# Device layouts, DRAM hops and pooling on VectorE in a hybrid decoder step on eight cores

## The chip, the cores and the metric

The kernel runs on all 8 cores of one Trainium2 chip, two dies of four cores each (cores 0 to 3 and 4 to 7). Every core does the same program on its own share of the batch: one prompt of 2048 tokens and 16 sample sequences of 4 tokens, together 2112 columns. The cores do not talk to each other. The metric is the device time in microseconds of the slowest core.

Executions come in two states. In the fast state all cores have nearly the same granted TensorE clock (0.95 to 0.99 of full speed here). In the slow state one die, or both, is granted less (down to 0.80) and the run takes 1 to 17% longer, whatever the kernel. A ratio is the mean time of one kernel's fast runs over that of the other's fast runs of the same rounds, so it is not quite the ratio of the medians that are quoted beside it.

## The reference, cut to what matters

Four layers. In each, one input projection feeds three branches. Branch A pools over trailing windows of 2, 4, 8 and 16 tokens. Branch B is a spatial gate, u * (W v + b), in chunks of 128 tokens. Branch C is a gated depthwise convolution of width 31 with a LayerNorm. The three are concatenated, go through one output projection, and a gated feed-forward network (FFN) with a depthwise convolution of width 3 follows.

```python
def pool_mix(xa, prev, pos0, w_pool, scale):
    xp = jnp.concatenate([prev, xa], axis=1).astype(jnp.float32)
    cs = jnp.concatenate([zeros, jnp.cumsum(xp, axis=1)], axis=1)
    for g, w in enumerate((2, 4, 8, 16)):                  # 64 channels each
        s = cs[:, P+1:P+1+T, sl] - cs[:, P+1-w:P+1-w+T, sl]
        outs.append(s / jnp.minimum(pos + 1, w))
    pooled = jnp.concatenate(outs, -1) - xp[:, P:]
    out = einsum('btgc,gcd->btgd', pooled, w_pool) * scale
    return out, xp[:, -P:]                                 # the new state: the last 15 rows, an output
# per layer (cut):
    c_in = zc[..., :D_C] * sigmoid(zc[..., D_C:])
    c_conv, cst = causal_dwconv(c_in, conv_prev[l], conv_w[l], conv_b[l])
    c_out = silu(layernorm(c_conv, ...))
    x = x + concat([a_out, b_out, c_out], -1) @ w_out[l]
    x = x + (silu(dwconv3(h2 @ w_gate)) * (h2 @ w_val)) @ w_down[l]
```

The states that a next step needs are outputs too: of pooling (15 rows), of the convolution (30 rows) and of the FFN convolution (2 rows), and the rows of v.

## The kernel before

Everything on the chip has channels on the 128 partitions and tokens in the free dimension. The convolution uses another layout (12 groups, 4 phases of 32 channels), so its input has to hop into that layout and its output back. A helper records every operation with what it reads and writes and places the waits; memory is handed out from one arena in which buffers overlay each other, so an operation can wait for a transfer that still reads the memory that it will overwrite. The parts that the argument touches:

```python
# conv input: 16 transfers from SBUF to SBUF for each third j of the channels
for q in range(4):
    for f in range(4):
        S.dma("sp", Q[32*f:32*f+32, 4*j+q, 8:8+MT], cin[32*q:32*q+32, j, f, :], DQ[j], reads=[Rcin[j]], writes=[Rq[j]])
# ... the last 94 tokens once more, with channels in the free dimension, for the state outputs (TensorE)
for k in range(KC):
    S.op("pe", lambda e: e.matmul(pt[0:94, 0:256], H[:, k, NT-94:NT], wv[:, k, 0:256], ...))        # L561
# ... 12 conv groups, sums for the LayerNorm (L601), LayerNorm on VectorE, with V matmuls (L633) between
# conv output: again 16 small transfers per third, then a GpSimd copy into token order (L671)
for f in range(4):
    S.dma("sp", cop[32*q:32*q+32, j, f, :], coq[32*f:32*f+32, :], DCO[j], reads=[Rys[g]], writes=[Rcp[j]])
# ... pooling: projection A (L718), then the window sum as matmuls of shifted operands (L744), with weights
# that GpSimd scales by the coefficient of each shift (L706): 4 shifts for one half, 16 for the other
for i in range(WMAX[j]):
    S.op("pe", lambda e: e.matmul(pb[:, 0:n], wpb[:, j, i, :], zab[:, j, 15+c0-i:15+c0-i+n], start=(i == 0), ...))
# ... 22 transposes of the FFN state (L782), then the spatial gate and U (L798, L812), then output projection (L838)
# ... FFN: per block of 128 channels, after the two groups of 8 matmuls per token tile (L893, L897), a small one
for k in range(KC):
    S.op("pe", lambda e: e.matmul(pt[0:66, 0:128], H[:, k, NT-66:NT], wv[:, k, 0:128], ...))        # L926
```

Inputs come in the reference's layouts, so x, the vectors and the states are transposed on TensorE at the start and y at the end; the spatial weights are masked and transposed at each layer boundary.

## Time and profile before

The median is 3372.56 us of 3 runs. I cut the slowest core's execution into stages by the start of the first matmul of each kind in the TensorE timeline:

| stage (us) | layer 1 | 2 | 3 | 4 |
|---|---|---|---|---|
| start to first projection | 85.7 | | | |
| conv input projection | 48.0 | 51.1 | 54.0 | 54.0 |
| conv | 48.1 | 48.3 | 47.9 | 48.3 |
| conv end to output projection | 114.4 | 114.0 | 114.2 | 113.9 |
| output projection | 83.1 | 83.1 | 83.1 | 83.1 |
| FFN up to the last down projection | 445.2 | 445.1 | 446.3 | 442.4 |
| last down projection to the next layer, or to the end | 67.4 | 66.5 | 66.7 | 116.6 |

The first lines are from the page of the kernel before: busy microseconds of TensorE with their share of the span, and the share of each engine in the chain of work that ended last.

```profile
PE 3099.0 (92%) x17856; PEld 1516.0 (45%) x17856; DVE 1706.6 (51%) x3064; ACT 1463.8 (43%) x2876; POOL 363.1 (11%) x460
...
PE 81%; DVE 5%; SPq 4%; issue 3%; ACT 2%; DMA 2%; POOL 1%; DVEq 0%; ACTq 0%; POOLq 0%
```

TensorE (PE) is the bound, so time goes only where its instructions or its gaps go. The next lines are the TensorE timeline of the kernel before around the start of the third layer's conv. The columns are start, duration, engine, line, operation, output and inputs, count, and in brackets how long the engine had stood before and what released it.

```profile
1756.38 2.10 PE L608 MATMUL ps<-arena 128*128 128x512 bf16 x9
...
1770.44 1.05 PE L601 MATMUL ps<-arena,oneb 128*128 128x512 bf16 x4 [11.74 <-DVE arena L620]
1771.34 4.00 PE L608 MATMUL ps<-arena 128*128 128x512 bf16 x9
```

TensorE stands 11.74 us, and the next nine matmuls take 4.00 us instead of 2.10: the restart is slow. The release names VectorE, but VectorE only passed on a wait. This is the ScalarE timeline of the same moment, and below it the queue of SyncE, which issues transfers.

```profile
1769.06 0.70 ACT L618 ACTIVATE arena<-ps,cvq_s 128x528 f32<-128x528 f32 x1 [14.30 <-DMA o_conv_s<-arena]
```

```profile
1739.85 25.16 SPq L134 DMA_DIRECT2D arena<-arena  x31
...
1765.68 1.96 SPq L134 DMA_DIRECT2D o_conv_s<-arena  x4
```

ScalarE had to wait for an output transfer that reads memory which it overwrites, and that transfer stood in the queue behind 31 hop transfers of 0.8 us of issue each. Now the stretch between conv and output projection of the third layer, again TensorE:

```profile
1824.32 12.49 PE L718 MATMUL ps<-H,wsall 128*128 128x512 bf16 x64
1844.35 3.94 PE L718 MATMUL ps<-H,wsall 128*128 128x512 bf16 x16 [7.54 <-ACT arena L721]
...
1858.02 16.15 PE L744 MATMUL ps<-arena 128*128 128x512 bf16 x80 [4.47 <-POOL arena L706]
1874.01 0.17 PE L767 MATMUL ps<-arena,pw 128*128 128x16 bf16 x1
...
1875.02 4.64 PE L782 MATMUL ps<-cstt,arena 32*128 32x32 f32 x22
```

The pooling matmuls (L744) and the state transposes (L782) are work that the change takes away, and 12 us are gaps. One more reading: a GpSimd copy and a VectorE operation that ran beside it, from the two engines' timelines.

```profile
1822.79 4.05 POOL L671 COPY arena<-arena 128x2048 bf16<-128x2048 bf16 x1 [32.42 <-DMA arena<-arena]
```

```profile
1823.23 4.18 DVE L657 TENSOR_TENSOR arena<-arena 128x528 f32<-128x528 f32 x1
```

The operation of L657 takes 0.70 us beside no copy. The Trainium skill, page "SBUF — State Buffer", section "Who interferes with whom", says that a VectorE instruction with two inputs in SBUF contends with a GpSimd instruction that reads SBUF; the 4.18 us agree.

### The profile page before, as it was taken

How to read it: one execution, taken by the hardware profiler on the slowest of the kernel's cores; microseconds unless marked ns; L12 is line 12 of the kernel's file. 1: busy time of each engine (PE TensorE's matmuls, PEld its weight loads, DVE VectorE, ACT ScalarE, POOL GpSimd, SP SyncE). 2: the span in 40 equal slices, each digit the busy share in tenths (PEclk: the TensorE clock that was granted, in tenths of full speed). 3: DMA queues.
4: the chain of work that ended last, by engine and by line, in shares of the span. 5: the costliest groups of instructions: out<-in, count | busy, mean ns of one | idle time of the engine just before them, and what ended most of it. 6: DMA issues, size and time to landing. Idle time of an engine off the chain costs nothing.

```text
span 3370.9 us, 53934 instructions; the slowest of 8 cores (3356.4 to 3370.9 us)
## 1 busy us (share of the span) xinstructions
PE 3099.0 (92%) x17856; PEld 1516.0 (45%) x17856; DVE 1706.6 (51%) x3064; ACT 1463.8 (43%) x2876; POOL 363.1 (11%) x460
## 2 busy tenths in 40 slices
PE   4889999999888999999878999999988899999995
PEld 3445444444344444444434544444434454444443
DVE  4234664645532475555543366464652347556455
ACT  4240662725342273545425147272732407536353
POOL 0120001000002010101012101010101200010100
PEclk8899999999998999999989999999998999999998
DMA  5522233333332233333152223333315213333312
GB/s 134 95 44 32 26 40 38 34 39 48 48 65 41 28 33 39 39 39 35 33 85 52 32 26 34 38 40 39 43 25 94 44 22 31 37 35 40 39 27 103
DMA packets 326036, 152.94 MB, mean 45 GB/s; under 512 B 229171, under 2 KB 312071, under 8 KB 325511
## 3 DMA queue, kind: packets, MB, share of 16 engines
q0 software_dynamic: 287232, 108.03, 28.2%
q1 hardware_dynamic: 38535, 41.48, 4.2%
q8 instruction: 151, 2.47, 0.3%
q14 instruction: 118, 0.97, 0.1%
HBM read 232.98 MB, written 14.75 MB: 73 GB/s over the span
## 4 chain that ended last, share of the span: by engine, by line
PE 81%; DVE 5%; SPq 4%; issue 3%; ACT 2%; DMA 2%; POOL 1%; DVEq 0%; ACTq 0%; POOLq 0%
PE ps L893 19%; PE ps L897 18%; PE ps L948 14%; PE ps L838 7%; PE ps L983 5%; SPq L134 4%; PE ps L812 4%; PE ps L608 3%; PE ps L542 2%; DVE H L379 2%; PE ps L546 2%; PE ps L744 2%; PE ps L367 1%; PE ps L926 1%; ACT arena L365 1%
## 5 line engine op out<-in xcount | busy, mean ns | idle before, releaser
L893 PE MATMUL ps<-H,wsall 128*128 128x512 bf16 (+1 forms) x3520 | 703.1, 343 | 0.0
L897 PE MATMUL ps<-H,wsall 128*128 128x512 bf16 (+1 forms) x3520 | 700.2, 342 | 0.0
L910 DVE SCALAR_TENSOR_TENSOR arena<-arena,vt 128x512 f32<-128x512 f32 (+1 forms) x440 | 288.9, 657 | 432.3 <-ACT arena L909 431.9
L905 ACT COPY arena<-ps 128x512 f32<-128x512 f32 (+1 forms) x440 | 224.4, 510 | 650.0 <-PE ps L893 643.6
L948 PE MATMUL ps<-arena,wsall 128*128 128x512 bf16 (+1 forms) x2560 | 458.3, 342 | 0.0
L893 PEld LDWEIGHTS ps<-H,wsall 128*128 128x128 bf16 x3520 | 305.1, 98 | 335.4 <-issue 3.9
L897 PEld LDWEIGHTS ps<-H,wsall 128*128 128x128 bf16 x3520 | 302.1, 98 | 332.3
L365 ACT ACTIVATE arena<-X 128x512 bf16<-128x512 f32 (+1 forms) x360 | 171.7, 543 | 527.8 <-PE ps L367 270.9
L909 ACT ACTIVATE arena<-ps,vt 128x512 f32<-128x512 f32 (+1 forms) x440 | 309.2, 703 | 65.4 <-DVE arena L912 0.9
L948 PEld LDWEIGHTS ps<-arena,wsall 128*128 128x128 bf16 x2560 | 216.1, 98 | 241.6
L951 DVE TENSOR_TENSOR X<-ps,X 128x512 f32<-128x512 f32 (+1 forms) x320 | 185.3, 596 | 257.2 <-PE ps L948 257.2
L912 DVE SCALAR_TENSOR_TENSOR arena<-arena,vt 128x512 f32<-128x512 f32 (+1 forms) x440 | 289.4, 658 | 46.9 <-DVE arena L910 1.4
L134 POOL DMA_DIRECT2D wsall<-w_up x176 | 154.0, 879 | 1231.1 <-PE ps L926 716.5
L919 DVE TENSOR_TENSOR arena<-arena 128x512 bf16<-128x512 bf16 (+1 forms) x440 | 258.9, 591 | 3.0 <-ACT arena L918 2.6
L838 PE MATMUL ps<-arena,wsall 128*128 128x512 bf16 (+3 forms) x1440 | 260.3, 341 | 0.0
L379 DVE SCALAR_TENSOR_TENSOR H<-X,vt,arena 128x512 bf16<-128x512 f32 (+1 forms) x320 | 209.4, 657 | 93.2 <-ACT arena L376 63.6
L915 ACT CAST arena<-ps 128x512 bf16<-128x512 f32 (+1 forms) x440 | 223.9, 509 | 72.1 <-PE ps L897 71.9
L918 ACT ACTIVATE arena<-arena 128x512 f32<-128x512 f32 (+1 forms) x440 | 246.1, 559 | 3.3 <-DVE arena L912 3.1
L983 PE MATMUL ps<-arena,wsall 128*128 128x512 bf16 (+1 forms) x960 | 184.7, 358 | 12.3 <-DVE X L986 9.3
L838 PEld LDWEIGHTS ps<-arena,wsall 128*128 128x128 bf16 (+1 forms) x1440 | 120.0, 97 | 134.1 <-issue 0.2
L367 PE MATMUL ps<-arena,ones 128*128 128x512 bf16 (+1 forms) x360 | 120.7, 375 | 58.7 <-ACT arena L365 39.5
L840 DVE TENSOR_TENSOR X<-ps,X 128x512 f32<-128x512 f32 (+1 forms) x160 | 91.5, 594 | 135.3 <-PE ps L838 130.3
(123 smaller groups left out, 2550.4 us busy)
## 6 DMA issues: line engine op xcount, KB each, us to landing
wsall<-w_up POOLq DMA_DIRECT2D x176, 256.0 KB, 5.0
wsall<-w_down POOLq DMA_DIRECT2D x32, 512.0 KB, 5.6
arena<-cwd POOLq DMA_DIRECT2D x48, 288.0 KB, 6.7
arena<-arena SPq DMA_DIRECT2D x384, 33.0 KB, 1.9
arena<-xp SPq DMA_DIRECT2D x4, 2048.0 KB, 15.1
y_p<-arena SPq DMA_DIRECT2D x16, 512.0 KB, 2.7
wsall<-w_in POOLq DMA_DIRECT2D x24, 256.0 KB, 6.5
wsall<-w_in POOLq DMA_DIRECT2D x8, 768.0 KB, 9.9
```

The costliest lines, as they stand in the source:

```text
L134: ins = st["eng"].dma_start(out=out, in_=in_, **kw)
L379: S.op("dve", lambda e: e.scalar_tensor_tensor(H[:, kc, c0:c0 + n], X[:, kc, c0:c0 + n], VT[:, gcol + kc:gcol + kc + 1], ri, ALU.mult, ALU ...
L838: S.op("pe", lambda e: e.matmul(pb[:, 0:n], lh, rh, start=(q == 0), stop=(q == 8)), reads=[RWS[sl], rr], writes=[Rpb], inc=(q == 8))
L893: S.op("pe", lambda e: e.matmul(pg[:, 0:n], wv[:, k, 0:128], H[:, k, c0:c0 + n], start=(k == 0), stop=(k == 7)), reads=[RWS[sl], RH[ti]], ...
L897: S.op("pe", lambda e: e.matmul(pv[:, 0:n], wv[:, k, 128:256], H[:, k, c0:c0 + n], start=(k == 0), stop=(k == 7)), reads=[RWS[sl], RH[ti]] ...
L909: S.op("act", lambda e: e.activation(T_, pg[:, 0:n], AF.Identity, bias=fb, scale=w2), reads=[Rpg, Rvt], writes=[Rtm[q]])
L910: S.op("dve", lambda e: e.scalar_tensor_tensor(T_, G[:, gc - sh:gc - sh + n], w1, T_, ALU.mult, ALU.add), reads=gr_ + [Rvt], writes=[Rtm[q]])
L912: S.op("dve", lambda e: e.scalar_tensor_tensor(T_, G[:, gc - 2 * sh:gc - 2 * sh + n], w0, T_, ALU.mult, ALU.add), reads=gr_ + [Rvt], write ...
L918: S.op("act", lambda e: e.activation(T_, T_, AF.Silu), reads=[Rtm[q]], writes=[Rtm[q]])
L919: S.op("dve", lambda e: e.tensor_tensor(actb[:, fl, c0:c0 + n], VB_, T_, ALU.mult), reads=[Rvst[q], Rtm[q]], writes=[Rab[ti]])
L948: S.op("pe", lambda e: e.matmul(pb[:, 0:n], wd[:, kk, m2 * 128:(m2 + 1) * 128], actb[:, kk, c0:c0 + n], start=(kk == 0), stop=(kk == nf - 1)),
L983: S.op("pe", lambda e: e.matmul(pb[:, 0:n], wvw[:, kk - k0, m * 128:(m + 1) * 128], actb[:, kk, c0:c0 + n], start=(kk == 0), stop=(kk == n ...
```

## The change

Its intent is to take everything off TensorE that is not the model's arithmetic. Inputs and outputs are brought on the host into the layouts that the chip uses, so the transposes and the matmuls that made channel-last state rows go. The conv hops go through DRAM (one write and four reads per third, instead of 16 small transfers). The window sums of the pooling become shifted additions on VectorE, over fp32, and only one matmul per tile is left. All weights come as one list of slabs (blocks that one transfer loads) in the order of use. The core of the diff:

```diff
-    o_pool_s = dout("o_pool_s", [DEPTH, 16, 15, D_A])
+    o_pool_s = dout("o_pool_s", [DEPTH, 128, 2, 16 * 15])
+    hop1 = nc.dram_tensor("hop1", [3, 128, 4 * MT], BF16).ap()
+    hop2 = nc.dram_tensor("hop2", [3, 128, 4 * MT], BF16).ap()
     ... cut: the other inputs and outputs, weight slabs, vectors, state and norm code ...
-                    for q in range(4):
-                        for f in range(4):
-                            S.dma("sp", Q[32 * f:32 * f + 32, 4 * j + q, 8:8 + MT], cin[32 * q:32 * q + 32, j, f, :], ...)
+                S.dma("sp", hop1[j], cin[:, j].rearrange("p f m -> p (f m)"), DH1[j], reads=[Rcin[j]], writes=[Rh1[j]])
+                h1v = hop1[j].rearrange("(q c) (f m) -> f c q m", q=4, f=4)
+                for f in range(4):
+                    S.dma("sp", Q[32 * f:32 * f + 32, 4 * j:4 * j + 4, 8:8 + MT], h1v[f], DQ[j], reads=[Rh1[j]], writes=[Rq[j]])
     ... cut: likewise hop2 (four writes and four reads per third) for the conv output; the GpSimd copies stay (L561) ...
+            for j in range(2):
+                out_dma(o_pool_p[l][:, j, :], zt[:, j, ZS - 15:ZS], [Rz[j]], f"pstg{j}")
+                out_dma(o_pool_s[l][:, j, :].rearrange("p (b i) -> p b i", b=16),
+                        zt[:, j, ZS:ZW].rearrange("p (b i) -> p b i", i=19)[:, :, 4:19], [Rz[j]], f"pstg{j}")
+            s_lo, Rs_lo = AR.carve("slo", 0, ZW, 1)          # scratch: overlays the conv output that hop2 reads
+            s_hi, Rs_hi = AR.carve("shi", YW - ZW, ZW, 1)
     ... cut: for half j, 2 or 4 additions of z shifted by 1, 2, 4, 8 (L588, L590) ...
+                steps.append((lambda e: e.scalar_tensor_tensor(P[:, 16:NP_], src[:, 31:ZS], iw, z[:, 31:ZS], ALU.mult, ALU.subtract),
+                              [Rsrc, Rcst], [RP[j], Rz[j]]))                            # L601, writes over z
-                            S.op("pe", lambda e: e.matmul(pb[:, 0:n], wpb[:, j, i, :], src, start=(i == 0), stop=(i == WMAX[j] - 1)), ...)
+                    S.op("pe", lambda e: e.matmul(pb[:, 0:n], PW[:, j, :], Pt[j][:, c0:c0 + n], start=True, stop=True), ...)
-    (L561, L926: the extra matmuls for the last tokens; L782 and others: transposes)
```

The line that this case turns on is the sixth addition: the sample state of pooling now leaves the chip as 16 pieces of 15 floats (60 bytes) per partition, packed one behind the other, 2048 pieces for each half j.

## The prediction

> **What bounds it now.** TensorE is busy 92% of 3371 us (page, part 1) and makes 81% of the chain that ended last (part 4). In the FFN stages it runs 8 matmuls of 512 columns in 1.73 us back to back (timeline), without gaps: those stages can only lose instructions. The rest to win is extra TensorE work and gaps in the mixer, at the start and at the end. Gaps cost twice: after them 8 such matmuls take 3.5 us for a while (timeline; the Trainium skill, "TensorE: Matmul & The Clock Gate", Part 1, tells of half the clock after an idle window).
>
> **What goes, from the TensorE timeline, third layer unless said:**
> 1. Start: first projection at 85.7 us, after vector and X transposes and mask building. Now X comes laid out: 8.65 MB plus 3.1 MB of weights at the 250 to 320 GB/s of the start's busiest windows is about 42 us; first projection near 46 us: -38.
> 2. Conv-state tail matmuls, 0.89 us x12: -11.
> 3. Conv: an 11.7 to 12.7 us gap per layer: ScalarE waits for an output DMA, queued behind 16 hop DMAs, whose buffer it overwrites; then a cold restart. The new buffer overlaps nothing: -14 x4 = -56.
> 4. FFN tail matmuls, 0.45 us x88: -40.
> 5. Mask work at layer boundaries, against the last layer, which lacks it (24.9 to 16.4 us): -8.5 x3 = -25.
> 6. End: 136 transposes and their buffer waits: -36.
> 7. From conv to out-projection: 114 us (V 22, A 24 with a 7.5 us wait for hop DMAs, pooling matmuls 20 and waits, state transposes 4.6, U 37). Pooling matmuls shrink to 2 us; A and V fill the LayerNorm.
>
> **What it adds (in 7).** VectorE gets six shifted adds of about 2365 fp32 columns and two combines of 2032 per layer. At (columns+150)/0.96 ns, which fits the 0.70 us of 528 columns here, this is about 23 us with small ones. They follow the LayerNorm (24 operations, 17 us) and precede U's bias adds. The first combine also waits until the pool-state output DMA, queued behind the hops, has read z. And three GpSimd copies of 3.7 us now fall here; one add that met such a copy took 4.18 instead of 0.70 us, in agreement with the Trainium skill, "SBUF — State Buffer", Who interferes with whom. I expect VectorE free about 60 us after the conv. TensorE has 36.6 us of A and V and about 8 us of U until PSUM is full, stands for 15 to 20 us, restarts cold and does 29 us more of U: about 95 instead of 114 us: -19 x4 = -76. Evictions of the pool matmuls: +6 in all.
>
> So VectorE becomes the mixer's limit. The DRAM hops replace 96 issues per layer by 39 and are hidden. Larger weight descriptors lower the DMA share, but weights were not the limit.
>
> Sum: 38+11+56+40+25+36+76-6 = 276. Predicted 3095 us, range 3040 to 3165. Faster by over 2%: 0.97; within 2%: 0.02; slower: 0.01.
>
> **Right if:** first projection near 46 us; no gap after the second conv group; FFN step 14.4 instead of 14.86 us; per layer a TensorE gap of 10 to 20 us in U, released by VectorE; TensorE busy about 2900 us.
>
> **Wrong if:** GpSimd does not block the adds, or pool outputs leave early (no gap, about 3040); the DRAM hops stall conv or out-projection; the start's DMA stays under 200 GB/s; denser TensorE work lowers the granted clock.

## The result

Fast runs of the changed kernel took 3178.32, 3178.52 and 3177.12 us; two more runs were slow (3355.02 and 3545.43 us, die 0 at a clock of 0.90 and 0.84). The ratio to before is 0.943 (95% interval 0.941 to 0.945). It is correct. The prediction, 3095 us with a range of 3040 to 3165, had the direction right and the size wrong: 194 us were gained on the slowest core, where 276 were expected; 3178 lies outside the range.

The same lines of the page, changed kernel:

```profile
PE 2872.8 (90%) x15915; PEld 1369.1 (43%) x16192; DVE 1757.1 (55%) x2987; ACT 1389.9 (44%) x2599; POOL 223.1 (7%) x436
...
PE 81%; DMA 6%; DVE 5%; issue 3%; ACT 2%; POOL 1%; SPq 1%; DVEq 0%; ACTq 0%; POOLq 0%
```

TensorE lost 226 us of work, but its share fell to 90%, and transfers (DMA) now hold 6% of the chain. Stage by stage (before core 5, after core 2; sums over the layers where there are four):

| stage | predicted | measured | difference |
|---|---|---|---|
| start to first projection (85.7 to 64.1) | -38 | -21.6 | +16 |
| conv input projection | -11 | -11.7 | -1 |
| conv (48.2 to 36.4 in the mean) | -56 | -47.2 | +9 |
| conv end to output projection (114.1 to 110.0 in the mean) | -70 (-76, +6 evictions) | -16.7 | +53 |
| output projection | 0 | 0 | 0 |
| FFN | -40 | -46.6 | -7 |
| layer boundary (66.9 to 62.5 in the mean) | -25 | -13.0 | +12 |
| end (116.6 to 80.0) | -36 | -36.6 | -1 |

One term is missing most of its size. Here is what TensorE does in that stretch of the third layer, changed kernel, in its timeline; conv ends at 1697.1.

```profile
1739.61 0.39 PE L633 MATMUL ps<-wt_s,arena 128*96 128x128 bf16 x4
1773.31 3.62 PE L645 MATMUL ps<-H,wsall 128*96 128x512 bf16 x8 [33.31 <-DVE arena L618]
```

It does the A and V projections and the first three groups of U without a gap, then stands 33.31 us and restarts at half the pace (3.62 us for eight matmuls that otherwise take 1.73 from one start to the next). That restart agrees with the Trainium skill, "TensorE: Matmul & The Clock Gate", Part 1. What VectorE does in that time:

```profile
1735.82 4.89 DVE L588 TENSOR_TENSOR arena<-arena 128x2366 f32<-128x2366 f32 x1 [11.61 <-DMA hop<-arena]
1740.90 2.68 DVE L590 SCALAR_TENSOR_TENSOR arena<-arena,cstt 128x2364 f32<-128x2364 f32 x1 [0.19 <-DVE arena L588]
...
1754.73 2.33 DVE L601 SCALAR_TENSOR_TENSOR arena<-arena,cstt 128x2032 bf16<-128x2032 f32 x1 [10.60 <-DMA o_pool_s<-arena]
...
1757.89 8.07 DVE L588 TENSOR_TENSOR arena<-arena 128x2366 f32<-128x2366 f32 x3
...
1772.51 0.55 DVE L618 COPY arena<-ps 64x384 f32<-64x384 f32 x1
```

VectorE is one queue in program order. The evictions that TensorE waits for (instructions that read a result out of PSUM, the memory that TensorE writes, and so free it for the next: L618 and the bias adds behind it) stand behind the pooling additions, as predicted. The additions themselves cost what was estimated (2.62 to 2.68 us for about 2365 columns). But VectorE stands twice: 11.61 us until the hop writes have read the memory that its scratch overlays, and 10.60 us until the pooling state has left, because L601 writes over z. So it reaches L618 75 us after the end of the conv, where the prediction had it free after about 60. The waits of the whole execution (total, number, longest), changed kernel:

```profile
PE ps L645 <- DVE arena L618: 137.6, 4, 37.0
...
DVE arena L601 <- DMA o_pool_s<-arena: 50.1, 4, 18.6
DVE arena L588 <- DMA hop<-arena: 43.3, 3, 15.9
```

And the transfers (size of one, and the median time from issue to landing):

```profile
o_pool_s<-arena SPq DMA_DIRECT2D x8, 120.0 KB, 14.6
```

120 KB in 14.6 us is 8 GB/s. The table of stretches shows the DMA engines in the wait; the columns are the stretch, its length, busy time of PE, PE weight loads, DVE, ACT and POOL with the number of instructions, the granted clock, the summed time of the packets as a share of 16 engines' time, and GB/s.

```profile
1744.00:1755.00 11.00, 0.00 (x0) 0.00 (x0) 0.40 (x2) 0.00 (x0) 4.92 (x4) 0.54 1.88 36
```

The packets fill 1.88 times the engines' time (they overlap) at 36 GB/s, while this core at other times moves above 150 GB/s. So two theories were open. **Theory A:** the small pieces of the pooling state are slow, hold the VectorE chain, and also slow the hops. **Rivals:** the additions on VectorE and the GpSimd copies that block them, the DRAM hops themselves, or the pooling on VectorE as such.

### The profile page after: what moved, and what is told of

Its sections match the earlier page's. It is cut to its first block, busy times and chain, and to the rows that moved or that the text cites. A ratio compares the mean times of both kernels' runs of the same rounds, so it can differ in the third digit from the quotient of the medians.

```text
span 3177.3 us, 48776 instructions; the slowest of 8 cores (3137.4 to 3177.3 us)
## 1 busy us (share of the span) xinstructions
PE 2872.8 (90%) x15915; PEld 1369.1 (43%) x16192; DVE 1757.1 (55%) x2987; ACT 1389.9 (44%) x2599; POOL 223.1 (7%) x436
## 4 chain that ended last, share of the span: by engine, by line
PE 81%; DMA 6%; DVE 5%; issue 3%; ACT 2%; POOL 1%; SPq 1%; DVEq 0%; ACTq 0%; POOLq 0%
PE ps L724 20%; PE ps L728 20%; PE ps L772 14%; PE ps L673 8%; PE ps L799 5%; PE ps L645 3%; PE ps L423 2%; PE ps L478 2%; PE ps L427 2%; DVE H L363 2%; DMA o_pool_s<-arena 2%; PE ps L351 1%; PE ps L505 1%; ACT arena L349 1%; DMA arena<-cwd 1%
## 5 line engine op out<-in xcount | busy, mean ns | idle before, releaser
L741 DVE SCALAR_TENSOR_TENSOR arena<-arena,vt_s 128x512 f32<-128x512 f32 (+1 forms) x440 | 288.7, 656 | 395.2 <-ACT arena L740 395.2
L772 PE MATMUL ps<-arena,wsall 128*128 128x512 bf16 (+1 forms) x2508 | 454.9, 341 | 2.7
L740 ACT ACTIVATE arena<-ps,vt_s 128x512 f32<-128x512 f32 (+1 forms) x440 | 309.3, 703 | 89.2 <-DVE arena L716 24.2
L743 DVE SCALAR_TENSOR_TENSOR arena<-arena,vt_s 128x512 f32<-128x512 f32 (+1 forms) x440 | 289.5, 658 | 46.6 <-DVE arena L741 0.9
L363 DVE SCALAR_TENSOR_TENSOR H<-X,vt_s,arena 128x512 bf16<-128x512 f32 (+1 forms) x320 | 209.4, 658 | 124.1 <-ACT arena L360 93.8
L645 PE MATMUL ps<-H,wsall 128*96 128x512 bf16 (+1 forms) x640 | 139.2, 364 | 137.6 <-DVE arena L618 137.6
L673 PE MATMUL ps<-arena,wsall 96*128 96x512 bf16 (+3 forms) x1416 | 258.9, 340 | 2.9 <-ACT arena L657 1.6
L799 PE MATMUL ps<-arena,wsall 128*128 128x512 bf16 (+1 forms) x944 | 180.1, 354 | 15.4 <-DVE arena L754 13.7
```

Source lines behind the costliest of these rows:

```text
L363: S.op("dve", lambda e: e.scalar_tensor_tensor(dst[:, kc, c0:c0 + n], X[:, kc, c0:c0 + n], VT[:, gcol + kc:gcol + kc + 1], ri, ALU.mult, A ...
L645: S.op("pe", lambda e: e.matmul(pU[0:96, 0:n], wvu[:, k, h * 96:(h + 1) * 96], H[:, k, c0:c0 + n], start=(k == 0), stop=(k == 7)), reads=[ ...
L673: S.op("pe", lambda e: e.matmul(pb[:, 0:n], lh, rh, start=(q == 0), stop=(q == 8)), reads=[RWS[sl], rr], writes=[Rpb], inc=(q == 8))
L740: S.op("act", lambda e: e.activation(T_, pg[:, 0:n], AF.Identity, bias=fb, scale=w2), reads=[Rpg, Rvt], writes=[Rtm[q]])
L741: S.op("dve", lambda e: e.scalar_tensor_tensor(T_, G[:, gc - sh:gc - sh + n], w1, T_, ALU.mult, ALU.add), reads=gr_ + [Rvt], writes=[Rtm[q]])
L743: S.op("dve", lambda e: e.scalar_tensor_tensor(T_, G[:, gc - 2 * sh:gc - 2 * sh + n], w0, T_, ALU.mult, ALU.add), reads=gr_ + [Rvt], write ...
```

## The experiments

All fourteen kernels gave correct results. Every edit is against the changed kernel, or against the version named. "Stage" is conv end to output projection, the mean of four layers on the profiled core.

### 1. rows: the pooling state leaves in whole rows

```diff
-    o_pool_s = dout("o_pool_s", [DEPTH, 128, 2, 16 * 15])
+    o_pool_s = dout("o_pool_s", [DEPTH, 128, 2, 16 * 19])
-                out_dma(o_pool_s[l][:, j, :].rearrange("p (b i) -> p b i", b=16), zt[:, j, ZS:ZW].rearrange("p (b i) -> p b i", i=19)[:, :, 4:19], ...)
+                out_dma(o_pool_s[l][:, j, :], zt[:, j, ZS:ZW], ...)     # 1216 bytes per partition; the host drops 4 of 19
```

> One edit: the pool state of the samples leaves as 128 whole rows of 1216 bytes per channel half instead of 2048 pieces of 60 bytes; same place in the queue. Theory A (the 60-byte pieces are what makes this output slow, 11 to 20 us to land, and VectorE's first combine waits for it): it lands in about 3 us, VectorE's wait for it falls from about 12.5 us per layer to under 3, TensorE's gap in U falls from about 33 us by 9 to 14 us per layer, time falls by 40 to 60 us to about 3125. Theory B (it is late because it is queued behind the hop DMAs, its size matters little): gain under 10 us. Theory C (VectorE's own work and the GpSimd copies make the gap): no gain.

Measured: 3118.7 us (fast runs 3115 to 3119), ratio to before 0.926 (0.924 to 0.927); stage 95.3 us instead of 110.0. The waits and the transfer, version rows:

```profile
PE ps L645 <- DVE arena L618: 81.1, 4, 22.7
...
DVE arena L588 <- DMA hop<-arena: 15.1, 4, 4.7
DVE arena L601 <- DMA o_pool_s<-arena: 13.8, 4, 4.9
```

```profile
o_pool_s<-arena SPq DMA_DIRECT2D x8, 152.0 KB, 3.8
```

More bytes landed in 3.8 instead of 14.6 us. Both waits of VectorE shrank, also the one for the hops (43.3 to 15.1 us), which were not touched. The cores' spans, 40 us apart in the changed kernel (3137 to 3177), lay within 11 us (3107 to 3118). The stage is now what the prediction had computed for it, 95 us, and for the reasons that it gave: in the third layer VectorE reaches L618 61 us after the end of the conv (about 60 predicted), and TensorE stands 19.58 us (15 to 20 predicted). Theory A holds for 60 of the 83 us that were missing.

### 2. early: the same 60-byte pieces, sent earlier

```diff
+                if g in (3, 7):          # before the second and third group of hop transfers, not after all hops
+                    pool_out(g // 4)     # the same two out_dma calls for half j
```

> One edit: the pool-state outputs keep their 60-byte pieces but are queued before the second and third hop groups, as soon as z is complete, instead of after all hops. Theory A (60-byte pieces): VectorE's combine no longer waits, but the hops behind these pieces take over 8 us more, so the GpSimd copies come later and the gain is less than with whole rows, 15 to 40 us. Theory B (queue place): the whole 40 us or more, hops as fast as before.

Measured: 3208.4 us, ratio 0.952 (0.951 to 0.954), slower than the changed kernel by 30 us; stage 118.6 us. The waits of version early:

```profile
POOL arena L567 <- DMA arena<-hop: 223.0, 11, 52.0
...
DVE arena L591 <- DMA hop<-arena: 130.2, 4, 33.1
```

The wait for the pieces is gone from the list, and the wait for the hops grew from 43.3 to 130.2 us. So theory A was right about the hops and wrong about the sum, which it had expected to be a gain of 15 to 40 us. Moving the pieces does not help: in this run the 1056-byte packets of the hops take 110 to 125 ns in the mean on every core, against 63 to 66 ns in rows.

### 3. start: the X tiles not held behind the constants

In the changed kernel the queue of SyncE shows why only the first X tile arrives early:

```profile
27.01 0.33 SPq L141 DMA_DIRECT2D cvq_s<-cvq  x1
27.38 15.77 SPq L141 DMA_DIRECT2D X<-xt  x4
```

The conv constants write into the same tracked resource as the vectors, so their transfer was issued only after the vectors had landed (25 us), and four X tiles stood behind it.

```diff
-                S.dma("sp", CVQ[:], cvq, DM["cvq"], writes=[Rvt])
+                S.dma("sp", CVQ[:], cvq, DM["cvq"], writes=[Rcv])      # and the three readers name Rcv
```

> One edit: the small load of conv vectors no longer waits for the landing of the other vectors, so the X loads behind it in the queue are issued at about 4 us instead of 27 us. If that wait is what made the start late, the first projection moves from 64.1 us to about 46 to 50 us and the time falls by 14 to 18 us. Rival: the start is bound by DMA bandwidth, and X and weights together take until 58 us anyway: first projection stays within 4 us of 64, no gain.

Measured: 3169.4 us, ratio 0.941 (0.939 to 0.943); first projection at 57.9 us. So 6 to 9 us, not the 14 to 18 that were missing. (In the other runs that leave the start as it was, the first projection of the profiled core lay between 60.3 and 66.2 us, so the size of this gain is rough.) The stretches from 1 to 28 us, first the changed kernel, then version start:

```profile
1.00:28.00 27.00, 0.00 (x0) 0.00 (x0) 0.73 (x7) 1.78 (x2) 3.34 (x6) 1.00 0.82 157
```

```profile
1.00:28.00 27.00, 0.00 (x0) 0.00 (x0) 0.73 (x7) 1.28 (x1) 3.33 (x6) 1.00 0.91 194
```

The engines are busy for 82 and 91% of the time at 157 and 194 GB/s; the prediction had taken 250 to 320 GB/s from the busiest windows of the kernel before, and had named a rate under 200 GB/s as a way to be wrong. The changed kernel reaches 273 and 311 GB/s from 30 to 40 and from 40 to 50 us. The first weight slabs share the engines with the first X tile; no run shows why the first 28 us are slower.

### 4. dgfirst: the U weights requested after the last conv weights

```diff
-                wload()                    # in the loop over j: slabs 5 to 7, the last of them U
+                if j < 2:
+                    wload()
...
+                if g + NDG == NG:          # after the last conv weight block was requested
+                    wload()
```

> One edit: the 1.5 MB load of the U weights is requested after the last conv weight block instead of before the fifth. If the fifth conv group's wait comes from standing behind that load, TensorE's wait for conv weights (1.8 to 2.6 us per layer, then a cold restart) vanishes, the conv stage falls from 36.4 us to about 33.5 us per layer, 10 to 14 us in all. Rival: the conv weight blocks are slow by themselves (7.8 us to land, buffer freed too late): no change.

Measured: 3169.4 us, ratio 0.941 (0.939 to 0.943); the conv stages sum to 135.3 instead of 145.4 us. As expected: this was most of the +9 us in the conv row of the table, a wait of TensorE for a conv weight block that queued behind a slab that was not needed yet.

### 5. rows64: as many pieces, 64 bytes each, aligned

The whole rows changed the number of pieces, their size and their place at once. This run keeps the number.

```diff
+    o_pool_s = dout("o_pool_s", [DEPTH, 128, 2, 16 * 16])              # was 16 * 15
+                out_dma(..., zt[...][:, :, 3:19], ...)                     # was 4:19: one dummy float ahead of the 15
```

> The changed kernel with one thing different: each of the 2048 pieces of one half's pooling state is 64 bytes instead of 60 and begins on a 64-byte boundary in memory (the dummy first element is cut off on the host). The number of pieces is as before, only their size and alignment differ. Theory A1 (the number of small packets is what costs: about 2048 packets of some 100 ns on 16 engines): the time stays near the changed kernel's 3178 us (3165 to 3180), and the conv end to first output-projection matmul stays near 109 us. Rival A2 (a write that covers no whole 64-byte unit is what costs[...]): the time falls most of the way to the whole-rows version, 3118 to 3140 us, and that stage falls to 95 to 100 us.

Measured: 3121.2 us, ratio 0.927 (0.925 to 0.929); stage 97.1 us. The number of pieces is not the cause. Theory A1, mine, fell.

### 6 and 7. pitch and off32: length or place

pitch writes 60 bytes at each 64-byte boundary (output `16 * 16`, destination `[:, :, 0:15]`). off32 writes 64 bytes, beginning 32 bytes after a boundary (output `16 * 17`, destination columns 8 to 264).

> The changed kernel with the pooling state written in 2048 pieces of 60 bytes per half as there, but each beginning on a 64-byte boundary in memory (the last 4 bytes of each 64 stay unwritten). The run with full aligned 64-byte pieces was as fast as whole rows (3122 us). Theory P (a piece that leaves part of a 64-byte unit unwritten is slow): the time stays near the changed kernel's 3178 us, conv end to output projection near 109 us. Rival Q (only a piece that crosses a 64-byte boundary is slow): the time falls to 3115-3130 us and the stage to 94-99 us.

> The changed kernel with the pooling state written in 2048 pieces of full 64 bytes per half, but each beginning 32 bytes after a 64-byte boundary, so that each covers the halves of two units. Theory P (part of a unit unwritten) and rival Q (crossing) both expect it slow: 3175 to 3215 us, P the more so since each piece touches two units in part. If it is instead as fast as the aligned pieces, 3115 to 3130 us, then the length of 60 bytes is the cause (for instance a length that is no multiple of 32 or 64), not the place.

Measured: pitch 3178 and 3153 us (two fast runs), ratio 0.939 (0.933 to 0.944), stage 113.0, 105.4, 102.0 and 103.7 us: slow. The first of the two runs is itself a little disturbed (die 1 at a clock of 0.958, die 0 at 0.969), and the profiled core lies on that die; on die 0 the stage is 99 to 104 us, and the undisturbed die of both slow runs took 3144 us. So pitch loses about half of what the changed kernel loses. off32 3119.9 us, ratio 0.925 (0.922 to 0.929), stage 95.0 us: fast. So crossing a 64-byte boundary does not hurt, and beginning on one is not enough. Theory Q fell, and P did in its form with 64 bytes, which had expected off32 to be slow.

### 8 and 9. off16 and p32: the unit

What was left: a piece that fills a 32-byte unit only in part is slow (R), or any piece shorter than 64 bytes is (S). off16 is off32 with 4 to 260 in place of 8 to 264: the same pieces, read from the same place on the chip and written 16 bytes nearer to the start. p32 writes each piece as two of 32 bytes, 64 bytes apart, each filling one unit:

```diff
+                for e8 in range(2):
+                    out_dma(o_pool_s[l][:, j, :].rearrange("p (b i) -> p b i", b=16)[:, :, 16 * e8:16 * e8 + 8],
+                            zt[:, j, ZS:ZW].rearrange("p (b i) -> p b i", i=19)[:, :, 3 + 8 * e8:11 + 8 * e8], ...)
```

> The kernel of the run with 64-byte pieces that begin 32 bytes after a 64-byte boundary (fast: 3119 us), with one number changed: the pieces begin 16 bytes after a boundary, so each covers one 32-byte unit whole and two units in half. Theory R (a unit of 32 bytes that a piece fills only in part is slow to write): the time goes up to the changed kernel's 3178 us or above (3155 to 3210), conv end to output projection to 102-118 us. Rival S (pieces shorter than 64 bytes are slow): the time stays at 3115 to 3125 us and the stage at 95 us.

> The changed kernel with the pooling state written in 32-byte pieces, twice as many as before (4096 per half), each filling one aligned 32-byte unit. Theory R (only units filled in part are slow): near the fast versions although there are twice as many packets, 3115 to 3140 us, stage 94 to 101 us. Rival S (pieces shorter than 64 bytes are slow): at least as slow as the 60-byte pieces, 3178 us or more, stage 109 us or more.

One of four runs of off16 and one of six of p32 were fast (3182.6 and 3120.2 us), so there is no interval. The undisturbed die of the slow runs tells the same: its slowest core took 3177 and 3180 us in two runs of off16, and 3120, 3117 and 3117 us in three of p32. The stage was 112.4 us on average for off16, and 95.6 for p32 (core 4, on the undisturbed die). The wait of VectorE and the transfer, version off16:

```profile
DVE arena L601 <- DMA o_pool_s<-arena: 56.8, 4, 21.3
```

```profile
o_pool_s<-arena SPq DMA_DIRECT2D x8, 128.0 KB, 14.8
```

and version p32 (core 4), with twice the number of pieces:

```profile
DVE arena L603 <- DMA o_pool_s<-arena: 23.4, 4, 6.4
```

```profile
o_pool_s<-arena SPq DMA_DIRECT2D x16, 64.0 KB, 4.7
```

The trace's packet records of the profiled cores (core 4 for p32) give it in one table (ns for one packet of that size; the place is counted from the start of the output tensor; the 60-byte rows contain 1024 packets of the prompt's pooling state too, which are 60 bytes in all versions):

| version | piece | begins at (mod 32) | packets | mean | 90th percentile | longest | 1056-byte hop packets, mean |
|---|---|---|---|---|---|---|---|
| changed kernel | 60 B | any multiple of 4 | 17408 | 64 | 173 | 2036 | 82 |
| pitch | 60 B | 0 | 17408 | 48 | 111 | 2707 | 73 |
| off16 | 64 B | 16 | 16384 | 73 | 211 | 2421 | 87 |
| off32 | 64 B | 0 | 16384 | 13 | 12 | 576 | 65 |
| rows64 | 64 B | 0 | 16384 | 10 | 11 | 55 | 65 |
| p32 | 32 B | 0 | 32768 | 8 | 9 | 232 | 65 |

Three versions write units of 32 bytes in part, and these are the slow ones; three write whole units, and these are fast, whether the piece has 32 or 64 bytes. pitch, where each piece leaves one unit incomplete and shares none with its neighbour, is the mildest of the three. Writing units in part is not slow by itself: the prompt's pooling state leaves in 60-byte pieces 120 bytes apart in all versions, 128 to a transfer, and on the profiled cores of rows64, off32 and p32 these packets took 10 to 12 ns in the mean. What is shown is for transfers of 2048 such pieces.

The last column is that of the slowest core, and the other cores add something. In the changed kernel, off16, start and dgfirst each pair of neighbouring cores (0 and 1, 2 and 3, and so on) has one core whose hop packets took 77 to 88 ns in the mean, and this is the one with the longer span; on its partner they took 62 to 66 ns. In rows, rows64, off32 and p32 they took 63 to 67 ns on every core. On core 2 of the changed kernel, third layer, the hop packets that began between 1723 and 1733 us took 192 ns in the mean, and the core issued its own pieces only at 1743 us. So in that layer it was not the core's own pieces that slowed its hops. In the changed kernel the stage is 108 to 110 us on the four cores with slow hops, 104 to 107 us on their partners, and about 95 us on all cores of rows.

The Trainium skill, "Collectives: The Full Stack", "Rules for kernel authors", asks for buffers aligned to 32 bytes and gives as reason that it "Prevents HW read-modify-write". It says so of collectives; these runs agree with the unit for plain DMA writes to DRAM. That a read-modify-write is the mechanism, no run here shows.

### 10. nocopy: rows without the GpSimd copies

```diff
-                        S.dma("sp", cop[32 * q:32 * q + 32], h2v[q], DCO[j], reads=[Rh2[j]], writes=[Rcp[0]])
-                    S.op("pool", lambda e: e.tensor_copy(cout[:, j, 0:NP_].rearrange("p (m f) -> p m f", f=4), ...))
+                        S.dma("sp", cout[32 * q:32 * q + 32, j], h2v[q], DCO[j], reads=[Rh2[j]], writes=[Rco[j]])
-                    ops += [(wo[:, 6 + j, ms], cout[:, j, c0:c0 + n], Rco[j]) for j in range(3)]
+                    ops += [(wo[:, 6 + j, ms], cmov(j, c0, n), Rco[j]) for j in range(3)]   # columns 1056 bytes apart
```

> The whole-rows version (3119 us), with the second hop landing directly in the buffer that the output projection reads, which then takes its moving operand with a stride; the six GpSimd copies per layer that reordered it are gone. Theory B (while a GpSimd copy runs, a VectorE operation with two SBUF inputs takes 4 to 5 us instead of 2.6): the additions of the pooling chain run at 2.3 to 2.7 us each, conv end to output projection falls from 95 to 83-90 us, and the time to 3075-3105 us, provided the strided operand costs the output projection nothing (83.1 us per layer). Rival: the copies overlap with waits that end later, and the stage stays at 93 to 97 us: 3112 to 3122 us. If the strided operand is slower to stream, the output projection stage grows beyond 83.1 us and says so by itself.

Measured: 3372.7 us, ratio 1.002 (1.000 to 1.004): the whole gain is gone. The stage did fall, to 90.9 us, and every shifted addition took 2.62 us (in rows, those that met a copy took 4.35 and 4.40), so theory B is right about the additions and worth some 4 us per layer, a little less than expected (83 to 90 us). But the output projection grew from 83 to 155 us. The groups of its matmuls (count, busy time and mean ns of one), versions nocopy and rows:

```profile
L672 PE MATMUL ps<-arena,wsall 128*128 128x512 bf16 x640 | 420.7, 798 | 0.0
```

```profile
L673 PE MATMUL ps<-arena,wsall 128*128 128x512 bf16 x640 | 159.2, 379 | 0.0
```

The 640 matmuls contain the 384 with the strided operand. The Trainium skill, "SBUF — State Buffer", under "Door 1", speaks of 16-byte lines and of a penalty for each access that goes to a new one, so that 8 bf16 can be strided over for free. Here neighbours are 1056 bytes apart, and the mean of the group is more than twice as long.

### 11. sbhop: rows with the hops from SBUF to SBUF, as before

```diff
-                S.dma("sp", hop1[j], ...)   # one write and four reads per third; likewise hop2
+                for q in range(4):
+                    for f in range(4):
+                        S.dma("sp", Q[32 * f:32 * f + 32, 4 * j + q, 8:8 + MT], cin[32 * q:32 * q + 32, j, f, :], ...)
```

> The whole-rows version (3119 us), with the hops between the two conv layouts done as in the kernel before: sixteen SBUF-to-SBUF transfers per third of the channels instead of a write to DRAM and a read back. It tells what the DRAM route is worth. Theory C (the route matters little, because the first conv group waits for the last projection's state and masks, and because packets are larger only by a factor of four): within 15 us of 3119, conv stage 36 to 40 us, gap before the first conv group up by at most 3 us per layer. Rival D (the DRAM route was what let the conv start early and end without gaps; the SBUF route's 11 us wait at the last group comes back): conv stage back to 44 to 48 us per layer, the time 3150 to 3170 us.

Measured: 3189.4 us, ratio 0.947 (0.945 to 0.949): 72 us slower than rows. Theory D was right that it would be slower, but it had expected 3150 to 3170 us, and it was wrong in place: the conv stages stay at 34 us, and the stage behind grows to 115.1. SyncE's queue and VectorE's timeline, third layer of sbhop:

```profile
1708.15 43.43 SPq L141 DMA_DIRECT2D arena<-arena  x48
```

```profile
1752.98 2.62 DVE L584 TENSOR_TENSOR arena<-arena 128x2366 f32<-128x2366 f32 x1 [28.02 <-DMA arena<-arena]
```

48 transfers take 43.43 us to issue, and the first addition stands 28 us until the last of them has read the memory that its scratch overlays. The DRAM route needs half the transfers. In the kernel before nothing on the chain waited so early for the hops out; with pooling on VectorE something does. The two parts of the change lean on each other.

### 12. pepool: rows with the pooling back on TensorE

The pooling code of the kernel before is put back into rows (100 matmuls per layer with weights scaled by GpSimd, instead of 10 matmuls after additions on VectorE).

> The whole-rows version (3119 us), with the pooling undone: windows are again summed by TensorE, as matmuls with shifted operands and weights that GpSimd scales, instead of shifted additions on VectorE. Theory E (with the small writes gone, the VectorE chain of about 13 additions still keeps TensorE waiting between the end of V and the pooling matmul, and the gap that it leaves is about as long as the matmuls that it removed, 100 matmuls or 17 to 20 us): conv end to output projection stays at 92 to 100 us and the time at 3105 to 3140 us. Rival F (moving the pooling to VectorE did save TensorE time that is on the critical path): the stage grows to 105 to 115 us and the time to 3160 us or more.

Measured: 3095.4 us, ratio 0.920 (0.918 to 0.922): 20 us faster than rows, although TensorE has more to do; stage 88.2 us. Neither theory had expected so short a stage; E was nearer. The stretches of the third layer's stage, first pepool, then rows:

```profile
1655.00:1743.00 88.00, 88.00 (x546) 49.03 (x544) 49.01 (x78) 33.13 (x64) 23.49 (x24) 1.00 0.25 61
```

```profile
1669.00:1764.00 95.00, 75.02 (x455) 42.78 (x454) 70.00 (x85) 27.14 (x49) 17.59 (x9) 0.89 0.25 61
```

pepool keeps TensorE busy for all of 88.00 us at full clock. rows has 13 us less work and 20 us of gap, and the clock falls to 0.89. Moving the pooling to VectorE was a loss of 7 us per layer in this order of instructions (20 us of time); what the stage gained over before came from the rest.

### 13 and 14. hybrid and best

pepool has no gap, rows has less work. hybrid takes both: windows 2 and 4 on TensorE (20 matmuls), 8 and 16 on VectorE (about 15 us of additions), scratch in memory that comes free earlier (with another order of the conv buffers), the copy of L618 on ScalarE, pooling outputs before the second read back. best adds the edits of start and dgfirst.

```diff
-            for j in range(2):
+            for j in (1,):                                   # VectorE: only the half with windows 8 and 16
                 for f, r_, w_ in pool_steps(j):
+            for ti, (c0, n) in enumerate(TTS):               # TensorE: windows 2 and 4, right after V
+                for i in range(4):
+                    S.op("pe", lambda e: e.matmul(pb[:, 0:n], wpb[:, i, :], zb[:, 15 + c0 - i:15 + c0 - i + n], ...))
-            S.op("dve", lambda e: e.tensor_copy(vs_v[0:64, 0:384], pb[0:64, 0:384]), ...)
+            S.op("act", lambda e: e.copy(vs_v[0:64, 0:384], pb[0:64, 0:384]), ...)
```

> The whole-rows version (3119 us) with the pooling split: the half with windows 2 and 4 is summed on TensorE (20 matmuls of a shifted operand, 3.8 us in the run with pooling on TensorE), the half with windows 8 and 16 on VectorE (15 us of additions), the additions' scratch buffers are moved to memory that comes free earlier, the value state is copied by ScalarE instead of VectorE behind the additions, and the pooling outputs leave before the second read back. Theory G (TensorE waits in this stage because VectorE is one queue, and the additions stand before the evictions of the spatial products): the 19.6 us gap shrinks to 2-8 us, conv end to output projection falls from 95 to 77-82 us and the time to 3050-3072 us. Rival: the wait moves to something else and the stage stays above 88 us, as with all pooling on TensorE (3099 us).

> The split pooling together with the two small repairs that were run alone: the X tiles not held behind the constants (worth 8 us) and the U weights requested after the last conv weights (worth 10 us). If the parts add: the split version's time less 15 to 20 us, 3030 to 3055 us, with first projection at about 58 us, conv stages at 33 to 35 us and conv end to output projection at 77 to 82 us. If conv end to output projection grows because the U weights come later, the sum is less by that.

Measured: hybrid 3059.3 us, ratio 0.907 (0.905 to 0.910), stage 80.8 us. best 3051.4 us (two fast runs of four), ratio 0.905 (0.902 to 0.908), stage 81.2 us, conv stages 33.5 us, first projection at 58.9. The parts add only in part: hybrid's conv stages already lay at 35.2 us instead of 37.3, so dgfirst had less left. TensorE in best, third layer, the one gap of the stage that is over 1 us:

```profile
1678.18 0.26 PE L690 MATMUL ps<-wts_s,arena 64*96 64x64 bf16 x1 [2.52 <-DVE arena L686]
```

hybrid changes five things at once, and the other four (scratch, copy on ScalarE, early outputs, order of the conv buffers) were not run without the split. So how much of the 59 us over rows the split itself is worth is not shown.

best is 9.5% faster than the kernel before and 4% faster than the changed kernel (the ratio of the two ratios, 0.905 over 0.943).

## Why the prediction was wrong, point by point

- **What bounds the kernel: right.** TensorE work and its gaps explain every stage. TensorE was predicted to be busy for about 2900 us; it was for 2873.
- **Extra matmuls (conv tail, FFN tail) and the end: right.** -11, -40 and -36 were predicted; -11.7, -46.6 and -36.6 came.
- **Conv gap: right, slightly large.** -56 predicted, -47.2 measured. No TensorE gap as long as the old one is left; a new wait for conv weights behind an early slab took about 10 us of it back, as dgfirst shows.
- **The failed step: "conv end to output projection about 95 instead of 114 us: -19 x4 = -76".** It came to 110.0 us. The mechanism in it was right: VectorE as one queue, additions ahead of U's evictions, a TensorE gap and a slow restart. The term that failed is "VectorE free about 60 us after the conv": it was 75 us in the third layer, and TensorE stood 33.31 us instead of 15 to 20. The prediction even named the wait of the first combine for the pool-state transfer, but gave it no time (10.60 us there), and took the hops for hidden (11.61 us of wait there). With that one transfer in whole 32-byte units the stage is 95.3 us (rows), 97.1 (rows64), 95.0 (off32) and 95.6 (p32). The 60-byte pieces cost about 15 us per layer, 60 in all: with whole rows the waits of VectorE for them fell from 50.1 to 13.8 us and those for the hops from 43.3 to 15.1, 64 us together on the profiled cores.
- **"The DRAM hops ... are hidden": wrong.** VectorE's first additions waited 43.3 us for them in the changed kernel, and still 15.1 us in rows, where no pieces slow them. They were worth having all the same: with the old hops rows is 72 us slower (sbhop).
- **"Pooling matmuls shrink to 2 us" as a gain: wrong in sign once the rest is repaired.** pepool, with the matmuls, is 20 us faster than rows.
- **Start: the mechanism right, the rate mis-sized.** 250 to 320 GB/s were taken from the busiest windows; 157 came at first, 194 with the false dependency removed. The term -38 measured -21.6. Some 6 to 9 of the missing 16 us were the false dependency; the rest stays open (the transfer rate and the norm chain, which the runs do not separate).
- **Layer boundary: the term mis-sized.** -25 predicted, -13.0 measured. The estimate compared with the last layer, which is followed by no projection. In the third layer after the change, the timeline shows TensorE stand 1.19 and 3.15 us in the first projections, behind VectorE's norm writes; I made no run on it, so the other part stays open.
- **GpSimd copies: right.** nocopy shows the additions at 2.62 us without copies; beside them they took 4.35 and 4.40 us in rows and 4.89 us in the changed kernel.
- **Denser work lowering the clock: did not happen.** Before 0.960 to 0.963 on the cores, after 0.963 to 0.968, best 0.976 to 0.982.

What stays open: by which mechanism a partly written unit is slow, whether it matters that two pieces share one, and how the pieces slow the hops. In four versions with partial units one core of each pair has slow hops (on core 2 of the changed kernel before its own pieces are issued, in three of the four layers), and the spans of the fast runs spread by 31 to 40 us; in early the hops are slow on all cores, and the spans spread by 8 to 19 us. That fits pieces of the partner core which write into a memory that both use, but no run separates the two cores.

## What to carry to other kernels

Where many small pieces go to DRAM, write whole aligned units: here 2048 60-byte pieces per transfer, or 64-byte pieces shifted by 16 bytes, cost about 60 us where the same number of 64-byte pieces, or twice as many of 32 bytes, cost nearly nothing, and padding the rows and cutting them on the host was enough. When work moves from the bound engine to another, ask in what order that other engine's queue then stands and which transfers its scratch memory must wait for: freeing TensorE of 13 us of work per layer bought a 20 us gap, and the version that split the work (with four smaller edits) was faster than either extreme. A small transfer that "is hidden" deserves its own number as soon as something on the chain writes over what it reads.

## What the Trainium skill lacked or had wrong

- "DMA: Bandwidth & Descriptors", "Rules for kernel authors", tells to coalesce many small transfers, and its section "Specifications" puts the size below which a read-modify-write happens at 512 bytes; neither gives a unit that a plain write to DRAM should fill. Here it mattered little that pieces were under 512 bytes: a transfer of 2048 pieces landed in 4.7 us with 32 bytes each and in 4.6 us with 64, but in 14.6 us with 60, where 32-byte units are written in part. As an alignment for the buffer, 32 bytes stands in "Collectives: The Full Stack", "Rules for kernel authors", but for collectives.
- No page says that partial-unit writes slow other transfers: in the changed kernel and off16 the 1056-byte hop packets had a mean of 79 to 88 ns on one core of each pair, and 62 to 67 ns on its partner and in the versions without such writes.
- "SBUF — State Buffer", "Who interferes with whom", names two factors of slowdown but not the sizes of the instructions that they belong to. Here a fp32 addition of 2366 columns took 4.35 to 4.89 us beside a GpSimd copy of 3.7 us and 2.62 us alone. The formula for fp32 additions on the page "VectorE: DVE Perf Modes", in its section on the TRN2 errata, gives 2.62 us and agrees.
- "SBUF — State Buffer", "Door 1", speaks of a penalty for strides above 16 bytes without its size for a matmul's moving operand: a group of which 384 of 640 matmuls have columns 1056 bytes apart had a mean of 798 ns instead of 379.
- "TensorE: Matmul & The Clock Gate", Part 1, tells to budget 13/16 of the clock for dense matmuls on three or more cores of a die. In fast runs on all eight cores the mean granted clock was 0.95 to 0.99; only the slow state, on one die or both, came near it, down to 0.80.
